# Latent attention: full-row rope scores on zero-padded keys, rotated queries by a second product, lag-table inputs on GpSimd, the softmax scale on the keys

## The chip, the cores and the metric

The kernel runs on one core of a Trainium2 chip. Its engines are TensorE (PE in the profile; its weight loads have rows of their own, PEld), VectorE (DVE), ScalarE (ACT), GpSimd (POOL) and SyncE (SP), whose queue issues most of the DMAs. The metric is device microseconds (us) of one execution; a kernel's time is the median of its runs.

## What is computed

The reference is a backbone of two layers over 512 latent tokens and 256 context tokens, 1024 features wide. Layer 0 is attention with 16 heads on a compressed key of 128 features and a rotary key of 64; layer 1 is a bidirectional diagonal state-space layer (S5) with a gated unit. Only the attention, and the part of the S5's preparation that runs beside it, are touched:

```python
scale = (MLA_NOPE + MLA_ROPE) ** -0.5
keys_lat = jnp.concatenate([ckv_l, _apply_rope(kr_l, cos, sin)], axis=-1)
keys_ctx = jnp.concatenate([ckv_c, kr_c], axis=-1)
q_pos  = jnp.concatenate([qa, _apply_rope(qr, cs[:, None], sn[:, None])], axis=-1)
q_free = jnp.concatenate([qa, qr], axis=-1)
s_all = jnp.concatenate([q_pos @ keys_lat.T, q_free @ keys_ctx.T], axis=-1)
p = jax.nn.softmax(s_all.astype(jnp.float32) * scale, axis=-1)
o = p[..., :s] @ ckv_l + p[..., s:] @ ckv_c
```

A latent query sees all 768 keys, the latent ones with rotated rope features and the context ones with plain ones; a context query sees the 256 context keys.

## The kernel before

**Precision.** Each float32 operand is split into a high and a low part (`split`, line 63: ACT copies, DVE subtracts), and a product is three matmuls (`mm3`, line 79: high by high, high by low, low by high).

**Attention.** Scores have queries on the partitions. A unit is 128 latent queries of one head, or its 256 context queries: five units a head, 80 units. For a unit of latent queries `score` (line 725) makes one group of five matmuls against 512 latent keys and one against 256 context keys; for one of context queries, two groups against 256 keys. In a group, lines 735 to 737 are the three products with the compressed key, line 738 is the rope product high by high, and line 739 the rope products high by low and low by high in one matmul, since the 64 rope features' high part lies in one half of the 128 partitions and their low part in the other (K1, K2 for the keys, `stack` for the queries). Line 738 therefore uses 64 partitions of both operands. `softmax` (line 741) takes the row maximum on DVE, multiplies it by minus the scale on ACT, takes the exponential on ACT with the scale, and divides, on DVE or ACT. `turn` transposes the probabilities on PE and splits them; `values` and `up_values` make the outputs.

**Queries.** `prep(h)` makes the operands of the next head in the units of the one before: `abs_steps` the compressed queries, and for every second head `rope_steps` (line 435) the rope queries of a pair of heads: one product `up`, an ACT copy to SBUF, eight DMAs on SP's queue that exchange blocks of 16 rows (`turn_rows`, line 423), three DVE operations with the cosine and sine tables, and splits.

**S5 beside the attention.** In units 1 to 51, 32 times (5 chunks in 8 units), `s5_chunk` (line 314) makes the state-out weights of four groups with six POOL products of 512 columns (lines 325 to 330), the inputs of the lag table with three DVE operations, a DVE memset and two ACT copies (lines 336 to 344), the lag table with 32 small matmuls (lines 348, 351), and stores it with eight DMAs on SP's queue (lines 357, 358). The inputs `cb` and the weights `wo` have two buffers each, `bk` one. From unit 52 on `win_early` (line 381) has POOL make 14 pieces of state-in weights: per piece two loads, six products (lines 372 to 377) and a store, in the buffers of `wo` and `pw`.

**Order.** The program is written in the order of the units; a scheduler (`schedule_with_timeline_sim`) puts the instructions of each engine and queue into an order by its own estimate of their times, and each engine runs its order strictly.

**After the attention** comes the output projection, whose weights `wload` loads through SP's queue (line 889).

Of the kernel before, what the change touches and what calls it, by code (L numbers as in the profile page):

```python
# [31 lines left out]
def hybrid_mla_s5(ctx, tc, I, O):  # L32
# [30 lines left out]
    def split(hi, lo, src):  # L63
        return act.copy(hi, src).ins, dve.tensor_sub(lo, src, f(hi)).ins  # L64
# [23 lines left out]
    def mod_steps(blocks, wt, ps, work, n):  # L88
        """rows of 512 columns of the modulation, block j in column group j: one step for each of the inputs' tiles"""
# [69 lines left out]
    def s5_params(take, mm):  # L159
# [102 lines left out]
        # (lam_bar - 1) / lam  # L262
# [16 lines left out]
        # powers: slot s holds lam_bar^s forward, lam_bar^(7-s) backward; state-in coefficients  # L279
        # coef * lam_bar * slot(7 - i), groups on the partitions, conjugated  # L280
# [33 lines left out]
    def s5_chunk(work, mm, c, pw, cci, half, dcol, eyek):  # L314
        """state-out weights and lag tables of groups 4c .. 4c+3"""
# [16 lines left out]
        # input weights of the lag table, the directions in separate columns  # L332
# [3 lines left out]
        dve.tensor_tensor(b1, bb, cci[:, 0:2, gs].rearrange("p r g -> p g r").unsqueeze(3).broadcast_to([P, 4, 2, 16]),  # L336
                          op=ALU.mult)
        dve.tensor_tensor(b2, bb[:, :, ::-1, :], cci[:, 2, gs].unsqueeze(2).unsqueeze(3).broadcast_to([P, 4, 2, 16]),
                          op=ALU.mult)
# [14 lines left out]
        act.copy(ks, o)  # L354
        dve.scalar_tensor_tensor(ks[:, 0:16], eyek, dcol[:, c:c + 1], ks[:, 0:16], op0=ALU.mult, op1=ALU.add)
# [25 lines left out]
    def win_early(tables, scratch, engs, more):  # L381
        """pieces made ahead and kept in DRAM: the last one is stored, the next one loaded, this one made"""
# [13 lines left out]
    # ================= layer 0: latent attention =================  # L396
    with ExitStack() as ctx_:
# [37 lines left out]
        def rope_steps(hp):  # L435
            st = {}

            def load():
                raw = qp(0)[:, :256]
                sp.dma_start(out=raw, in_=I["uqr"][hp])  # L440
                st["w"] = lw[0]("whi"), lw[0]("wlo")
                split(*st["w"], raw)
# [3 lines left out]
            def up(a, b):  # L446
                wh, wl = st["w"]
                o = lmm[0](b - a)
                for kc in range(2):
                    k = slice(kc * P, (kc + 1) * P)  # L450
                    mm3(o, wh[:, k], wl[:, k], Qh[kc][:, a:b], Ql[kc][:, a:b], kc == 0, kc == 1)
# [15 lines left out]
            def turned():  # L467
                (_, p0), (_, p1) = ropes[hp]
                q, t = st["q"], st["t"]
                dve.tensor_mul(q, q, cs[:, 0, :])  # L470
                dve.tensor_mul(t, t, cs[:, 1, :])
                dve.tensor_add(q, q, t)
                stack(q, p0, p1, slice(0, TL))
            return [plain, plain_ctx, turned]

        def abs_steps(h):
            st = hd.setdefault(h, {})

            def fold():
# [3 lines left out]
                split(*st["u"], wa[:, 384:512])  # L483
# [23 lines left out]
        with mkpool(name="in_h", bufs=KC) as hp, mkpool(name="in_w", bufs=3) as wp, \  # L507
# [5 lines left out]
            lmm[0], lw[0] = mm, lambda n: wp.tile([P, 1024], F32R, name=n)[:, :256]  # L513
# [14 lines left out]
            def mod_part(q):  # L528
                """shift and scale of 256 features, the even and the odd tiles of the inputs apart"""
# [74 lines left out]
            def rms(tiles, cols, n):  # L604
                """RMSNorm over the partitions of the tiles, in place"""
# [55 lines left out]
            dve.tensor_add(kr[:, 0:TL], kr[:, 0:TL], tmp)  # L661
            next(gate0)
# [5 lines left out]
            dve.tensor_copy(Ch, ckv)  # L668
            dve.tensor_sub(Cl, ckv, f(Ch))
            for j in range(2):  # L670
# [4 lines left out]
                split(Vh[:, 3 * j:3 * j + 3, :], Vl[:, 3 * j:3 * j + 3, :], tp)  # L675
            for i in range(2):
# [15 lines left out]
            def mod_more():  # L692
                """a step of the products with the modulation weights, and the loads for the next one"""
# [19 lines left out]
        with mkpool(name="at_s", bufs=2) as work, mkpool(name="at_p", bufs=2, space=PSUM) as ps, \  # L713
# [5 lines left out]
            lmm[0], lw[0] = mm, lambda n: work.tile([P, 256], F32R, name=n, bufs=1)  # L719

            # a unit is 128 latent queries of a head, or its 256 context queries
# [3 lines left out]
            def score(i):  # L725
# [3 lines left out]
                half, kx, kh = (lo_, K2, K1) if h % 2 == 0 else (up_, K1, K2)  # L729
# [741 lines left out]
```

## Time and profile before

| | |
|---|---|
| three runs | 1840.08, 1857.38, 1853.53 us; median 1853.53 us |
| profiled execution | span 1848.7 us from its first to its last instruction; no other time of it is given |
| busy in the span | PE 1653.3 us (89%), DVE 1137.1 (62%), ACT 694.6 (38%), POOL 683.2 (37%) |
| chain that ended last | PE 53%, DVE 21%, DMA 14%, ACT 3%, POOL 3% of the span |
| attention | from 265 us (first score, line 735) to 765 us (last product of `up_values`) |
| gates before it | 110 to 264 us |

The busy share is an average over stages: POOL works mainly in the attention and in the S5, DVE hardest in the attention. The chain goes back from the last instruction, at each step to what released it; its shares say which engine or transfer was last, not how busy it was. An engine's idle time counts only where something behind it waits. Matmuls are pipelined and their ends are modelled, so their cost is read from the distance of their starts.

### The profile page before, as it was taken

Reading aid. Unit: us, or ns where it says so; the run is one execution under the profiler, and the core shown is the slowest. Engines: PE = TensorE matmul, PEld = TensorE weight load, DVE = VectorE, ACT = ScalarE, POOL = GpSimd, SP = SyncE. Lnnn points to the kernel's source line nnn. Section 1 sums busy time; section 2 is a strip of 40 time slices with the busy share of each in tenths; the row PEclk is TensorE's granted clock in tenths of the full one; section 3 lists DMA queues with packets and bytes.
Section 4 is the critical chain, followed back from the end, with each engine's and each line's share of the span. In section 5 each row is a group of like instructions: output and inputs, shape, how many; then the busy total and the mean of one; then the engine's idle time right before and its main releaser. Section 6 shows DMA issues by size and latency. Waiting matters only on the chain.

```text
span 1848.7 us, 26973 instructions
## 1 busy us (share of the span) xinstructions
PE 1653.3 (89%) x9754; PEld 1321.5 (71%) x9754; DVE 1137.1 (62%) x2356; ACT 694.6 (38%) x1415; POOL 683.2 (37%) x788
## 2 busy tenths in 40 slices
PE   7999998888988989987899875687979999999997
PEld 4755787766766767766779765565768888888876
DVE  3864448888899677735551499998844332333347
ACT  2511226465565646611334332233454222222220
POOL 0000017666776477445105664626770000000022
PEclk8999999899999989998999887888989999999999
DMA  9366412222222455467647755339995333333352
GB/s 324 99 211 203 112 52 88 74 92 83 85 70 90 136 164 166 145 204 219 202 133 211 165 134 153 119 91 266 258 288 156 129 108 105 112 98 119 105 180 68
DMA packets 144244, 268.82 MB, mean 145 GB/s; under 512 B 39760, under 2 KB 74848, under 8 KB 143984
## 3 DMA queue, kind: packets, MB, share of 16 engines
q1 hardware_dynamic: 126256, 258.69, 46.9%
q10 hardware_dynamic: 17792, 8.39, 1.6%
q8 instruction: 77, 1.26, 0.3%
q14 instruction: 55, 0.45, 0.1%
q0 software_dynamic: 64, 0.03, 0.0%
HBM read 215.39 MB, written 49.30 MB: 143 GB/s over the span
## 4 chain that ended last, share of the span: by engine, by line
PE 53%; DVE 21%; DMA 14%; ACT 3%; issue 3%; POOL 3%; SPq 1%; DVEq 0%; ACTq 0%; POOLq 0%
PE mm L80 13%; PE mm L81 13%; PE mm L82 13%; DMA wraw<-in_wout_dram 3%; DVE st L1141 3%; DVE rt L1138 3%; DMA pt<-pind 3%; DVE st L1140 2%; DVE rt L1139 2%; PE modps L102 2%; PE sc L739 2%; PE sc L738 2%; DVE wlo L64 2%; DMA toe<-kd 2%; PE tr L775 2%
## 5 line engine op out<-in xcount | busy, mean ns | idle before, releaser
L64 DVE TENSOR_TENSOR wlo<-wraw,whi 128x1024 fp32r<-128x1024 f32 (+1 forms) x155 | 184.2, 1190 | 349.1 <-ACT whi L64 347.8
L64 ACT CAST whi<-wraw 128x1024 fp32r<-128x1024 f32 (+1 forms) x155 | 148.9, 962 | 467.5 <-PE mm L81 302.9
L81 PE MATMUL mm<-st,whi 128*128 128x512 f32 x512 | 201.6, 394 | 0.0
L80 PE MATMUL mm<-st,whi 128*128 128x512 f32 x512 | 201.3, 393 | 0.4 <-DVE t L1250 0.4
L82 PE MATMUL mm<-st,wlo 128*128 128x512 f32 x512 | 198.9, 388 | 0.0
L1333 POOL TENSOR_TENSOR x<-x,row_g 128x1024 f32<-128x1024 f32 x4 | 9.6, 2402 | 426.2 <-DMA x<-x1d 387.1
L80 PE MATMUL mm<-h,whi 128*128 128x512 f32 (+1 forms) x384 | 142.7, 372 | 11.6 <-DVE gg L1178 7.1
L325 POOL TENSOR_TENSOR wt<-cb,pw 128x512 f32<-128x512 f32 x32 | 36.3, 1133 | 301.5 <-DVE mx L752 268.3
L82 PE MATMUL mm<-h,wlo 128*128 128x512 f32 (+1 forms) x384 | 140.1, 365 | 6.4 <-DVE wlo L64 6.4
L81 PE MATMUL mm<-h,whi 128*128 128x512 f32 (+1 forms) x384 | 140.2, 366 | 0.8 <-DVE h L1034 0.8
L1093 PE MATMUL mm<-u,pt 128*128 128x96 f32 x512 | 73.1, 307 | 54.9 <-DMA u<-ud 36.5
L80 PEld LDWEIGHTS mm<-st,whi 128*128 128x128 f32 x512 | 96.1, 188 | 23.6 <-PE mm L82 0.8
L1093 PEld LDWEIGHTS mm<-u,pt 128*128 128x128 f32 x512 | 70.0, 221 | 58.2 <-issue 34.6
L82 PEld LDWEIGHTS mm<-st,wlo 128*128 128x128 f32 x512 | 96.1, 188 | 21.5
L81 PE MATMUL mm<-hl,whi 128*128 128x512 f32 (+1 forms) x320 | 109.9, 345 | 0.4 <-DVE hl L570 0.4
L81 PEld LDWEIGHTS mm<-st,whi 128*128 128x128 f32 x512 | 96.3, 188 | 19.1
L80 PE MATMUL mm<-hh,whi 128*128 128x512 f32 (+1 forms) x320 | 108.2, 346 | 1.7 <-ACT whi L64 1.7
L82 PE MATMUL mm<-hh,wlo 128*128 128x512 f32 (+1 forms) x320 | 108.9, 344 | 0.2 <-DVE wlo L64 0.2
L372 POOL TENSOR_TENSOR t<-pt,bt 128x512 f32<-128x512 f32 x14 | 20.8, 1488 | 223.8 <-DMA pt<-pind 177.4
L749 DVE TENSOR_REDUCE mx<-sc 128x1 f32<-128x768 f32 (+1 forms) x96 | 74.0, 772 | 37.4 <-PE sc L739 37.3
L775 PE MATMUL tr<-ident,p 128*128 128x128 f32 x448 | 72.2, 283 | 26.3 <-DVE ptl L64 22.7
L80 PEld LDWEIGHTS mm<-h,whi 128*128 128x128 f32 x384 | 75.4, 197 | 24.3 <-DVE gg L1178 7.9
(350 smaller groups left out, 4532.8 us busy)
## 6 DMA issues: line engine op xcount, KB each, us to landing
wraw<-in_wglu_dram SPq DMA_DIRECT2D x64, 512.0 KB
wraw<-in_win_dram SPq DMA_DIRECT2D x52, 512.0 KB
wod<-wo SPq DMA_DIRECT2D x32, 512.0 KB
wo<-wod SPq DMA_DIRECT2D x32, 512.0 KB
pt<-wid SPq DMA_DIRECT2D x24, 512.0 KB
u<-ud SPq DMA_DIRECT2D x32, 384.0 KB
pt<-pind SPq DMA_DIRECT2D x18, 512.0 KB
bt<-in_Bc_dram SPq DMA_DIRECT2D x18, 512.0 KB
```

The lines of the kernel that those rows point to most:

```text
L64: return act.copy(hi, src).ins, dve.tensor_sub(lo, src, f(hi)).ins
L80: pe.matmul(ps, lh, rh, start=first, stop=False)
L81: pe.matmul(ps, lh, rl, start=False, stop=False)
L82: pe.matmul(ps, ll, rh, start=False, stop=last)
L102: pe.matmul(mps[32 * j:32 * j + 2, :], sT[:, kc, :], w, start=(kc == 0), stop=(kc == KC - 1))
L738: pe.matmul(o, xr[half, ts], kh[half, a:b], start=False, stop=False)
L739: pe.matmul(o, xr[:, ts], kx[:, a:b], start=False, stop=True)
L749: dve.reduce_max(mx[:, 0:1], s, axis=AX.X)
L775: pe.transpose(tp[:, n, :], p[:, j * P:(j + 1) * P], ident)
L1093: pe.matmul(o[:, r, 96 * q:96 * (q + 1)], wi[:, q, r, :], us[m][:, 4 * (c % 2) + q, :], start=True, stop=True)
L1138: eng.tensor_tensor(t1, st[:, :, :, k], lr, op=ALU.mult)
L1141: eng.tensor_tensor(st[:, :, :, k + 1], st[:, :, :, k + 1], t2, op=ALU.add)
```

## The change

- The scale is multiplied into the rotary key and, after its use as value, into the compressed key. `softmax` takes the negated maximum on DVE and has no ACT multiplication.
- Two tiles KZ hold the high part of the rotary key in one half of the partitions and zeros in the other; line 738 becomes a matmul over all 128 partitions.
- The weights of the rope queries are stored twice in DRAM, as they are and with the blocks of 16 features exchanged. The rotated queries are a second product `up(0, TL, True)`; the copy to SBUF and the eight DMAs a pair of heads go, and the three DVE operations and the splits read PSUM. The load of these weights is twice as wide (512 columns).
- The low parts of the rope weights and of the head's value weights are made by POOL (`split(..., pool)`).
- In `s5_chunk` the two products of the lag table's input go to POOL, and two POOL additions of 64 partitions write `bk`, of which there are two, zeroed once. `half` and the two ACT copies go. The lag table's copy leaves out its first 16 columns, which DVE takes from PSUM.

```diff
+    def split(hi, lo, src, eng=None):
+        return act.copy(hi, src).ins, (eng or dve).tensor_tensor(lo, src, f(hi), op=ALU.subtract).ins
...
-        dve.tensor_tensor(b1, bb, cci[:, 0:2, gs]..., op=ALU.mult)
-        dve.tensor_tensor(b2, bb[:, :, ::-1, :], cci[:, 2, gs]..., op=ALU.mult)
-        dve.tensor_tensor(b1, b1, b2, op=ALU.add)
-        bk = work.tile([P, 4, 2, 48], F32, name="bk", bufs=1)
-        dve.memset(bk[:, :, :, 32:48], 0.0)
-        for d in range(2):
-            act.activation(bk[:, :, :, 16 * d:16 * d + 16], b1, AF.Copy, scale=half[:, d:d + 1])
+        pool.tensor_tensor(b1, bb, cci[:, 0:2, gs]..., op=ALU.mult)
+        pool.tensor_tensor(b2, bb[:, :, ::-1, :], cci[:, 2, gs]..., op=ALU.mult)
+        bk = bks[c % 2]
+        for d, rows in enumerate((lo_, up_)):
+            pool.tensor_tensor(bk[rows, :, :, 16 * d:16 * d + 16], b1[rows], b2[rows], op=ALU.add)
...
-        act.copy(ks, o)
-        dve.scalar_tensor_tensor(ks[:, 0:16], eyek, dcol[:, c:c + 1], ks[:, 0:16], op0=ALU.mult, op1=ALU.add)
+        act.copy(ks[:, 16:P], o[:, 16:P])
+        dve.scalar_tensor_tensor(ks[:, 0:16], eyek, dcol[:, c:c + 1], o[:, 0:16], op0=ALU.mult, op1=ALU.add)
...
             def load():
-                raw = qp(0)[:, :256]
+                raw = qp(0)
                 sp.dma_start(out=raw, in_=I["uqr"][hp])
-                split(*st["w"], raw)
+                split(*st["w"], raw, pool)
...
-                st["q"], st["t"] = qp(1), qp(0)
+                st["q"] = qp(1)
                 o = up(0, TL)
-                act.copy(st["q"], o)
-                turn_rows(st["t"], st["q"])
-                stack(st["q"], f0, f1, slice(0, TL))
+                stack(o, f0, f1, slice(0, TL))
+                dve.tensor_mul(st["q"], o, cs[:, 0, :])
...
-                q, t = st["q"], st["t"]
-                dve.tensor_mul(q, q, cs[:, 0, :])
-                dve.tensor_mul(t, t, cs[:, 1, :])
-                dve.tensor_add(q, q, t)
-                stack(q, p0, p1, slice(0, TL))
+                o = up(0, TL, True)
+                dve.tensor_mul(o, o, cs[:, 1, :])
+                dve.tensor_add(o, o, st["q"])
+                stack(o, p0, p1, slice(0, TL))
...
-                split(*st["u"], wa[:, 384:512])
+                split(*st["u"], wa[:, 384:512], pool)
...
+            dve.tensor_scalar_mul(kr, kr, SCALE)
...
-            dve.tensor_copy(Ch, ckv)
-            dve.tensor_sub(Cl, ckv, f(Ch))
...
+            dve.tensor_scalar_mul(ckv, ckv, SCALE)
+            dve.tensor_copy(Ch, ckv)
+            dve.tensor_sub(Cl, ckv, f(Ch))
...
-                half, kx, kh = (lo_, K2, K1) if h % 2 == 0 else (up_, K1, K2)
+                kx, kz = (K2, KZ[0]) if h % 2 == 0 else (K1, KZ[1])
...
-                    pe.matmul(o, xr[half, ts], kh[half, a:b], start=False, stop=False)
+                    pe.matmul(o, xr[:, ts], kz[:, a:b], start=False, stop=False)
...
-                    dve.reduce_max(mx[:, 0:1], s, axis=AX.X)
-                    act.mul(mx[:, 1:2], mx[:, 0:1], -SCALE)
-                    act.activation(p[:, a:b], s, AF.Exp, bias=mx[:, 1:2], scale=SCALE, accum_out=mx[:, 2:3])
+                    dve.reduce_max(mx[:, 1:2], s, axis=AX.X, negate=True)
+                    act.activation(p[:, a:b], s, AF.Exp, bias=mx[:, 1:2], scale=1.0, accum_out=mx[:, 2:3])
...
+            KZ = [work.tile([P, T], F32R, name=f"kz{i}", bufs=1) for i in range(2)]
+            for kz, k, rows, rest in ((KZ[0], K1, lo_, up_), (KZ[1], K2, up_, lo_)):
+                pool.memset(f(kz)[rest], 0.0)
+                act.copy(kz[rows], f(k)[rows])
+            bks = [work.tile([P, 4, 2, 48], F32, name=f"bk{i}", bufs=1) for i in range(2)]
+            for bk in bks:
+                pool.memset(bk, 0.0)
...
-    A["uqr"] = cont(ur.reshape(2, P, 8, P).transpose(2, 1, 0, 3).reshape(8, P, 256))
+    ur = ur.reshape(2, P, 8, 8, 16)
+    ur = np.stack([ur, ur[:, :, :, np.arange(8) ^ 1]], 0)
+    A["uqr"] = cont(ur.transpose(3, 2, 0, 1, 4, 5).reshape(8, P, 512))
```

## Rows read from the trace of the kernel before

**Rows 1.** Windows: stretch, length; busy PE, PEld, DVE, ACT, POOL; clock; DMA share, GB/s.
```profile
110.00:264.00 154.00, 153.77 (x761) 100.85 (x760) 67.10 (x188) 34.73 (x71) 0.00 (x0) 1.00 0.49 143
264.00:600.00 336.00, 296.40 (x2478) 233.32 (x2478) 291.67 (x545) 189.94 (x527) 235.03 (x192) 0.95 0.26 84
600.00:765.00 165.00, 152.89 (x949) 122.92 (x948) 113.40 (x227) 95.79 (x249) 113.74 (x85) 0.95 0.51 150
```

**Rows 2.** Timeline of PE's matmuls in the second unit: start, duration, what.
```profile
267.68 0.40 PE L736 MATMUL sc<-Cl,qd 128*128 128x512 f32 x1
267.91 0.39 PE L737 MATMUL sc<-Ch,qd 128*128 128x512 f32 x1
268.23 0.49 PE L738 MATMUL sc<-K,xp 64*128 64x512 f32 x1
268.65 0.50 PE L739 MATMUL sc<-K,xp 128*128 128x512 f32 x1
268.99 0.28 PE L735 MATMUL sc<-Ch,qd 128*128 128x256 f32 x1
269.11 0.28 PE L736 MATMUL sc<-Cl,qd 128*128 128x256 f32 x1
269.22 0.28 PE L737 MATMUL sc<-Ch,qd 128*128 128x256 f32 x1
269.43 0.38 PE L738 MATMUL sc<-K,t 64*128 64x256 f32 x1
269.75 0.38 PE L739 MATMUL sc<-K,t 128*128 128x256 f32 x1
269.97 0.27 PE L487 MATMUL mm<-wmod 128*128 128x128 f32 x1
```

**Rows 3.** The same windows view, from POOL's first to its last S5 product.
```profile
271.20:601.00 329.80, 290.20 (x2448) 229.43 (x2448) 289.93 (x541) 187.65 (x521) 235.91 (x192) 0.95 0.25 81
```

**Rows 4.** Groups by line, POOL: busy, mean ns, idle before and its releasers.
```profile
L327 POOL TENSOR_TENSOR wo<-wt,wt 128x512 f32<-128x512 f32 x32 | 42.9, 1340 | 55.5 <-issue 36.4 <-PE mm L351 14.3 <-DMA wod<-wo 2.0
...
L325 POOL TENSOR_TENSOR wt<-cb,pw 128x512 f32<-128x512 f32 x32 | 36.3, 1133 | 301.5 <-DVE mx L752 268.3 <-DMA cb<-in_CB_dram 31.5
```

**Rows 5.** Groups by line, POOL: its smaller products and sums in layer 1.
```profile
L1125 POOL TENSOR_TENSOR tr<-tr,trb 128x256 f32<-128x256 f32 x8 | 6.8, 856 | 0.5
...
L1128 POOL TENSOR_TENSOR tr<-tr,tr 128x128 f32<-128x128 f32 x8 | 3.7, 462 | 0.5
...
L1123 POOL TENSOR_TENSOR tr<-tr,lamt 128x128 f32<-128x128 f32 x8 | 3.3, 417 | 0.5
```

**Rows 6.** Groups by line, DVE: the operations of `s5_chunk`.
```profile
L340 DVE TENSOR_TENSOR b<-b,b 128x128 f32<-128x128 f32 x32 | 27.7, 867 | 0.3
...
L338 DVE TENSOR_TENSOR b<-cb,cci 128x128 f32<-128x128 f32 x32 | 23.5, 736 | 0.1
...
L355 DVE SCALAR_TENSOR_TENSOR ks<-eyek,dcol,ks 128x16 f32<-128x16 f32 x32 | 22.9, 715 | 0.7 <-ACT ks L354 0.5
...
L336 DVE TENSOR_TENSOR b<-cb,cci 128x128 f32<-128x128 f32 x32 | 22.5, 703 | 0.8 <-ACT bk L344 0.8
```

**Rows 7.** View of single lines: duration ns min/median/max, first and last start.
```profile
L336 DVE TENSOR_TENSOR b<-cb,cci x32: 278/607/1377, 272.7 to 596.6; 128x128 f32<-128x128 f32 x32
...
L426 SPq DMA_DIRECT2D modrow<-modrow x64: 507/587/1522, 229.8 to 704.9; - x64
...
L430 ACT CAST t<-modrow x8: 605/622/641, 229.6 to 700.5; 64x512 fp32r<-64x512 f32 x8
```

**Rows 8.** Timeline of POOL: first and last product of the 14 pieces.
```profile
615.42 1.29 POOL L372 TENSOR_TENSOR wt<-wo,pw 128x512 f32<-128x512 f32 x1 [14.54 <-DMA kd<-ks]
...
761.73 1.31 POOL L377 TENSOR_TENSOR wo<-pw 128x512 f32<-128x512 f32 x1
```

**Rows 9.** Timeline of SP's queue at the end of the attention.
```profile
763.06 0.33 SPq L386 DMA_DIRECT2D wid<-wo  x1
763.44 1.25 SPq L889 DMA_DIRECT2D wraw<-in_wout_dram  x2
```

More of the change, by code (lines that the diff above doesn't have):

```diff
@@ L61, in hybrid_mla_s5 @@
     pool.dma_start(out=nrm, in_=I["nrm"])
-    def split(hi, lo, src):
-        return act.copy(hi, src).ins, dve.tensor_sub(lo, src, f(hi)).ins
+    def split(hi, lo, src, eng=None):
+        return act.copy(hi, src).ins, (eng or dve).tensor_tensor(lo, src, f(hi), op=ALU.subtract).ins
     def wsplit(wp, src, n=1024):
@@ L312, in s5_params, with s5_chunk @@
             sp.dma_start(out=lamd[:, l], in_=lt[l])
-    def s5_chunk(work, mm, c, pw, cci, half, dcol, eyek):
+    def s5_chunk(work, mm, c, pw, cci, bks, dcol, eyek):
         gs = slice(4 * c, 4 * c + 4)
@@ L335, in s5_chunk @@
         bb = cb[:, :, :, 16:32]
[L336 to L339, printed above, removed]
[L340 to L344 removed]
+        pool.tensor_tensor(b1, bb, cci[:, 0:2, gs].rearrange("p r g -> p g r").unsqueeze(3).broadcast_to([P, 4, 2, 16]),
+                           op=ALU.mult)
+        pool.tensor_tensor(b2, bb[:, :, ::-1, :], cci[:, 2, gs].unsqueeze(2).unsqueeze(3).broadcast_to([P, 4, 2, 16]),
+                           op=ALU.mult)
+        bk = bks[c % 2]
+        for d, rows in enumerate((lo_, up_)):
+            pool.tensor_tensor(bk[rows, :, :, 16 * d:16 * d + 16], b1[rows], b2[rows], op=ALU.add)
         o = mm(P)
@@ L438, in load, with up @@
             def load():
-                raw = qp(0)[:, :256]
+                raw = qp(0)
                 sp.dma_start(out=raw, in_=I["uqr"][hp])
                 st["w"] = lw[0]("whi"), lw[0]("wlo")
-                split(*st["w"], raw)
+                split(*st["w"], raw, pool)
                 ropes[hp] = [(t768(F32R), ls.tile([P, TL], F32R, name=f"xp{e}", bufs=2))
                              for e in range(2)]
-            def up(a, b):
-                wh, wl = st["w"]
+            def up(a, b, turn=False):
                 o = lmm[0](b - a)
                 for kc in range(2):
-                    k = slice(kc * P, (kc + 1) * P)
-                    mm3(o, wh[:, k], wl[:, k], Qh[kc][:, a:b], Ql[kc][:, a:b], kc == 0, kc == 1)
+                    k = (kc + 2 * turn) * P
+                    wh, wl = (w[:, k:k + P] for w in st["w"])
+                    mm3(o, wh, wl, Qh[kc][:, a:b], Ql[kc][:, a:b], kc == 0, kc == 1)
                 return o
@@ L717, in mm @@
                 return ps.tile([P, 512], F32, name="mm")[:, :n]
-            lmm[0], lw[0] = mm, lambda n: work.tile([P, 256], F32R, name=n, bufs=1)
+            lmm[0], lw[0] = mm, lambda n: work.tile([P, 512], F32R, name=n, bufs=1)
             units = [(h, u) for h in range(HEADS) for u in range(5)]
@@ L794, in up_values @@
                 un[i].clear()
-            half = work.tile([P, 2], F32, name="half", bufs=1)
-            sp.dma_start(out=half, in_=I["half"])
+            KZ = [work.tile([P, T], F32R, name=f"kz{i}", bufs=1) for i in range(2)]
[5 more added lines that the diff above has]
+                pool.memset(bk, 0.0)
             dcol = work.tile([P, NCH], F32, name="dcol", bufs=1)
@@ L829, in hybrid_mla_s5 @@
                 if 5 * i // 8 < n_s5 <= NCH:
-                    s5_chunk(work, mm, n_s5 - 1, pw, cci, half, dcol, eyek)
+                    s5_chunk(work, mm, n_s5 - 1, pw, cci, bks, dcol, eyek)
                 if i == len(units) - 8:
@@ L1429, in lay_out @@
     A["Bc"] = cont(b.transpose(3, 1, 2, 0))
-    half = np.zeros((P, 2), np.float32)
-    half[:64, 0] = 1
-    half[64:, 1] = 1
-    A["half"] = half
     dc = np.zeros((4, 2, 16, 32), np.float32)
```

2 lines of the change are left out of this document (1 added, 1 removed).

## The prediction

> **What bounds the kernel now.** I read the windows of the stages first. Before the attention PE is busy all the time (153.8 of 154.0 us, clock 1.00), and POOL does nothing. In 264 to 600, with the 32 S5 chunks, PE is busy 296 of 336 us, DVE 292, POOL 235: three engines near their limit. From 600 to 765 PE is (153 of 165 us), with DVE at 113 and POOL at 114 [rows 1].
>
> How much of PE's busy time is work is read from the timeline, by the starts. The three compressed-key products of a 256-column group start 0.12 us apart, those of a 512-column group 0.23. Line 738, with 64 partitions, starts 0.21 after line 737, line 739 starts 0.32 after 738, and the next matmul 0.22 after 739. With 512 columns these are 0.32, 0.42 and 0.34 [rows 2]. The 64-row matmul breaks the pipeline at its entry and exit.
>
> Third, POOL's groups. Between its first and its last S5 product lie 329.8 us, 235.9 of them busy [rows 3]. The rest is mainly 55.5 us at line 327, for a free `wo` buffer that PE's lag-table matmuls or a store release late, and 31.5 us for `cb` loads [rows 4]. So POOL is paced by the others today, with 94 us to spare.
>
> **The change part by part.**
>
> *Full-row scores.* Three steps of a 256-column group are 0.21 + 0.32 + 0.22 = 0.75 us and would be 3 x 0.12 = 0.36 as full-row neighbours: 0.39 saved. With 512 columns 0.32 + 0.42 + 0.34 = 1.08 against 0.69: 0.39 again [rows 2]. There are 64 groups of 512 (four units in 16 heads) and 64 + 32 = 96 of 256: 160 x 0.39 = 62 us of PE, 0.78 a unit.
>
> The row shows a full-row weight load hidden behind the matmul before it: line 736 starts 0.12 us after 735 with other weights' load between them [rows 2]. The Trainium skill, TensorE: Matmul & The Clock Gate, section Part 3 (The mechanism), says the opposite: a weight load overlaps matmuls in flight only where the row groups differ. By that rule full rows would be no shorter; the trace disagrees, and the sum goes by the starts.
>
> *Second product.* Six 512-column matmuls at 0.23 [rows 2]: 1.4 us for each of 8 pairs of heads, 11 us of PE. The 64 exchange DMAs at 0.59 us [rows 7] leave SP's queue: 38 us of issue, counted at nothing, as what stands behind them there (chunk stores, weight loads) waits mostly for other things. The wider load of rope weights is one DMA as before, a unit ahead.
>
> *DVE and ACT.* The three operations of the lag table's input are 27.7 + 23.5 + 22.5 = 74 us of DVE in the 292 [rows 1, 6]. One takes 0.28 us at its shortest, 0.61 at the median, 1.38 at most [rows 7], the excess being about one POOL operation of 1.1 [rows 4]: it waits for POOL. ACT loses the maximum's multiplication, two copies a chunk and one a head pair; it was at 190 of 336 [rows 1], so nothing is counted. What DVE's relief is worth lies in PE's waits, which POOL now caps, so it gets no term of its own.
>
> *POOL.* Each chunk gets four operations: two products and two sums, 128 columns. Nearest rows: 0.42 and 0.46 us; lowest bound a quarter of a 512-column one, 0.28; highest a 256-column one, 0.86 [rows 4, 5]. I take 0.42, 0.42, 0.46, 0.46 = 1.76, which is 56 us for 32 chunks (36 to 110). The low parts of weights add, while the chunks run, 11 heads x 0.42 and 5 pairs x 1.13 [rows 4, 5]: 10 us. POOL's work in the chunks is then 235.9 + 56 + 10 = 302 us. The wait at line 327 goes, since POOL is now late and PE early. Of the 31.5 us for `cb`, which queue on SP behind the lag-table stores, between none and all may stay; I take a third, 10, as the stores come sooner after their chunk when PE and DVE are early. Chunk stretch: 312 in place of 330, **18 us less**. PE's own work there falls by 52 x 0.78 - 5 x 1.4 = 34 us of 296, DVE's by 74 of 292, so both fit below POOL. POOL is late next.
>
> The Trainium skill, GPSIMD Engine Reference, section Engine selection, keeps two-input elementwise work on VectorE, being about twice as fast there. The rows agree only where DVE waits for nothing (0.28 against 0.42). By the rule the move would cost 0.14 an operation; here DVE's mean is 0.70 to 0.87.
>
> *After the chunks.* The 28 units left save PE 28 x 0.78 = 22 us less two products (2.8): 19. With the 18 above PE would end 37 us sooner. POOL's 14 pieces, however, take from 615.4 to 763.0, paced by loads and stores [rows 8]; behind 18 us of gain they get 5 x 0.42 + 2 x 1.13 = 4 us of weight parts: POOL ends 14 us sooner. The output projection's first weight loads stand in SP's queue 0.4 us behind the last piece's store [rows 9]. Bounds 14 and 37. I take the middle, **25 us less**, since head 0's operands are made beforehand and only some of what follows needs POOL's buffers.
>
> *Before the attention.* One second product, 1.4 us, falls where PE has no gaps [rows 1]. KZ can be written only when the stage's space is free; its copy of 64 x 768 is nearest to 0.62 us for 64 x 512 [rows 7], about 0.9, and PE has three matmuls (0.7) to cover it: 0 to 3 us, taken as 1.5. The scalings and the later split of the key lie beside PE's gate products, DVE being busy 67 of 154 [rows 1]: nothing; uncovered, three 768-column operations, 3 us. Together **3 us more**.
>
> Sum: 25 - 3 = 22 us less. The profiled span, 1848.7, lies 4.8 under the median; I take that distance as fixed: 1853.5 - 22 = **1831**. From the bounds of its terms (POOL 0.28 to 0.5 an operation, `cb` 0 to 20, end 14 to 37) this case's own range is 1816 to 1843.
>
> **The rivals.**
>
> *A. PE's saving comes through whole.* The scheduler lets the S5 chunks slip behind the units, and the output projection starts without POOL's last piece. For it: PE needs POOL only for the chunks' small matmuls. Against: each engine's order is strict. PE's 62 - 11 = 51 us less 3: 1805; with fewer waits on DVE some 10 more, 1795.
>
> *B. Nothing comes of it.* All 31.5 us of `cb` waits stay (302 + 31.5 = 333, +3), and POOL's pieces gate the end (+4), plus 3: 1853 + 10 = 1863; with half of the waits, 1848. For it: POOL's idle time before a chunk is of that kind [rows 4]; against: SP issues less.
>
> *C. Slower: POOL's small operations are dear.* Strides, 64-partition outputs and waiting for DVE bring one to 0.86 [rows 5]. The chunks then take 235.9 + 110 + 10 + 31 = 387 us, PE waits at line 348 for `bk`, and against 22 us saved later 387 - 330 + 3 - 19 = 41 remain: 1895. It decides from 0.6 an operation with all `cb` waits. Against: the same instruction was 0.42 to 0.46.
>
> *D. The rope matmuls get no shorter*, their weight loads staying exposed as today. PE then keeps its 296 us in the chunks and its 153 after them, and 11 us of products are added: 1853 to 1868 with the 3 us from before the attention. Rows 2 speak against it. It is what the rule named above from the Trainium skill (TensorE: Matmul & The Clock Gate, Part 3) would give.
>
> **How the numbers follow.** Forecast 0.47, A 0.25, B 0.17, C 0.07, D 0.04. About 1% (18.5 us) is what a measurement of this kernel can tell from no change. The forecast lies just past it: of its 0.47 I put 0.31 beyond and 0.16 within. Faster 0.31 + 0.25 = 0.56; within 1% 0.16 + 0.16 + 0.04 = 0.36; slower, C and a corner of B, 0.08. The range leaves out C and the far ends of A and B: 1798 to 1858.
>
> **What would show it.** Line 738 as 128 rows, with 0.12 and 0.23 between starts. Small POOL operations near 0.45 us; POOL over 90% busy while the chunks run, its wait at line 327 nearly gone, and PE waiting for it at line 348. DVE's share there under 70%. POOL's last piece 10 to 20 us sooner, at 743 to 753, and PE at the end of the attention waiting on what stands behind it. Wrong it would be if POOL still waits at line 327 (A), if `cb` waits grow (B), or if the small operations exceed 0.6 (C).

## The result and the profile after

The changed kernel takes 1807.62 us (median; 1801.37 to 1812.57, four runs) beside 1849.91 us for the kernel before on the same chip: ratio 0.976, 95% interval 0.973 to 0.979, some 42 us less. The forecast was 22 less, 1831. The direction holds, and so does the whole range (1798 to 1858); the size was half, and the time lies below the 1816 to 1843 that the forecast's own terms allowed. The profiled execution, 1805.28 us with a span of 1803.5, is 45.2 us shorter than the one before (span 1848.7).

Where those 45 us lie is read from five marks in both traces:

| stretch | before | after | gained | forecast |
|---|---|---|---|---|
| start to POOL's first S5 product | 271.2 | 268.3 | 2.9 | -3 |
| POOL's first to last S5 product | 329.8 | 297.0 | 32.8 | 18 |
| from there to the first output product whose weights `wload` brings (`whi`, line 80) | 167.4 | 158.0 | 9.4 | 7 |
| from there to the end | 1080.3 | 1080.2 | 0.1 | 0 |

First the windows of the same stages; the columns are those of [rows 1]:

```profile
110.00:262.00 152.00, 151.34 (x768) 101.25 (x768) 66.57 (x186) 34.26 (x70) 2.48 (x3) 1.00 0.49 147
262.00:566.00 304.00, 272.68 (x2623) 235.35 (x2624) 200.18 (x426) 172.93 (x420) 290.18 (x339) 0.99 0.29 94
566.00:720.00 154.00, 123.44 (x848) 111.32 (x839) 95.85 (x197) 80.62 (x192) 112.54 (x90) 0.90 0.53 153
...
268.30:565.30 297.00, 266.61 (x2582) 230.47 (x2581) 197.12 (x422) 168.43 (x413) 287.09 (x335) 0.99 0.28 90
```

The last row answers to [rows 3]. In this stretch PE and DVE were both 88% busy before, POOL 72%. Now POOL is at 97% (287 of 297 us), PE at 90% and DVE at 66%; PE's granted clock rose from 0.95 to 0.99. After the chunks PE is busy only 123 of 154 us.

PE's timeline, answering to [rows 2]:

```profile
268.92 0.39 PE L735 MATMUL sc<-Cl,qd 128*128 128x512 f32 x1
269.15 0.40 PE L736 MATMUL sc<-Ch,qd 128*128 128x512 f32 x1
269.38 0.39 PE L737 MATMUL sc<-kz,xp 128*128 128x512 f32 x1
269.61 0.40 PE L738 MATMUL sc<-K,xp 128*128 128x512 f32 x1
269.85 0.28 PE L734 MATMUL sc<-Ch,qd 128*128 128x256 f32 x1
269.96 0.28 PE L735 MATMUL sc<-Cl,qd 128*128 128x256 f32 x1
...
270.20 0.28 PE L737 MATMUL sc<-kz,t 128*128 128x256 f32 x1
270.32 0.28 PE L738 MATMUL sc<-K,t 128*128 128x256 f32 x1
```

The steps are 0.23 us with 512 columns and 0.12 with 256, as forecast. Between lines 736 and 737 the weights change from those of a compressed query to those of a rope query, and nothing is lost.

POOL's groups by line while the chunks run, answering to [rows 4, 5]:

```profile
L327 POOL TENSOR_TENSOR wo<-wt,wt 128x512 f32<-128x512 f32 x32 | 41.5, 1297 | 0.8
...
L325 POOL TENSOR_TENSOR wt<-cb,pw 128x512 f32<-128x512 f32 x32 | 36.6, 1142 | 4.2 <-DMA cb<-in_CB_dram 2.1
...
L342 POOL TENSOR_TENSOR bk<-b,b 64x128 f32<-64x128 f32 x64 | 30.3, 474 | 2.4
L336 POOL TENSOR_TENSOR b<-cb,cci 128x128 f32<-128x128 f32 x32 | 14.7, 459 | 0.9 <-DMA cb<-in_CB_dram 0.9
L338 POOL TENSOR_TENSOR b<-cb,cci 128x128 f32<-128x128 f32 x32 | 12.9, 402 | 0.0
```

The wait at line 327 fell from 55.5 to 0.8 us, that for `cb` from 31.5 to 3.0 (2.1 at line 325, 0.9 at line 336), and the four small operations are 0.40 to 0.47 us. Now PE waits for POOL at line 346 (view of waits: total, times, longest):

```profile
PEld mm L346 <- POOL wo L330: 18.6, 21, 2.0
...
PE mm L346 <- POOL wo L330: 13.1, 15, 1.8
```

After the chunks POOL's 14 pieces still stand last, and SP's weight loads behind them, as in [rows 8, 9]; first POOL's timeline, then SP's, then the longest waits from 566 to 720:

```profile
716.58 1.32 POOL L375 TENSOR_TENSOR wo<-pw 128x512 f32<-128x512 f32 x1
```

```profile
717.93 0.32 SPq L384 DMA_DIRECT2D wid<-wo  x1
718.30 1.25 SPq L893 DMA_DIRECT2D wraw<-in_wout_dram  x2
```

```profile
POOL wt L370 <- DMA wo<-pind: 25.9, 11, 4.5
...
PE mm L82 <- POOL ul L64: 16.9, 2, 13.1
```

### The profile page after: what moved, and what is told of

The parts are those of the page before. It is cut to its first block, busy times and chain, and to the rows that moved or that the text cites. A ratio compares the mean times of both kernels' runs of the same rounds, so it can differ in the third digit from the quotient of the medians.

```text
span 1803.5 us, 26884 instructions
## 1 busy us (share of the span) xinstructions
PE 1603.7 (89%) x9802; PEld 1318.2 (73%) x9802; DVE 1029.4 (57%) x2206; ACT 662.8 (37%) x1249; POOL 738.9 (41%) x944
## 4 chain that ended last, share of the span: by engine, by line
PE 48%; DMA 20%; DVE 14%; POOL 10%; issue 4%; ACT 3%; SPq 1%; DVEq 0%; POOLq 0%; ACTq 0%
PE mm L80 13%; PE mm L81 13%; PE mm L82 13%; DMA wraw<-in_wout_dram 5%; DMA wo<-pind 3%; DMA pt<-pind 3%; DVE st L1145 2%; DMA toe<-kd 2%; DVE st L1144 2%; DVE rt L1142 2%; PE modps L102 2%; DVE wlo L64 2%; DVE rt L1143 2%; DMA wid<-wo 1%; DMA wraw<-in_win_dram 1%
## 5 line engine op out<-in xcount | busy, mean ns | idle before, releaser
L1097 PE MATMUL mm<-u,pt 128*128 128x96 f32 x512 | 79.0, 323 | 52.1 <-DMA u<-ud 30.7
L1097 PEld LDWEIGHTS mm<-u,pt 128*128 128x128 f32 x512 | 75.8, 236 | 55.4 <-issue 29.3
L80 PEld LDWEIGHTS mm<-st,whi 128*128 128x128 f32 x512 | 96.1, 188 | 23.7 <-PE mm L82 0.8
L749 ACT ACTIVATE p<-sc,mx 128x768 f32<-128x768 f32 (+1 forms) x96 | 73.8, 768 | 50.0 <-DVE mx L748 49.5
L64 POOL TENSOR_TENSOR ul<-wmod,uh 128x128 fp32r<-128x128 f32 x16 | 7.7, 481 | 199.3 <-ACT uh L64 199.2
L80 PE MATMUL mm<-whi,vh 128*128 128x512 f32 x186 | 72.9, 416 | 16.9 <-ACT whi L64 15.8
```

The source lines that it names most:

```text
L64: return act.copy(hi, src).ins, (eng or dve).tensor_tensor(lo, src, f(hi), op=ALU.subtract).ins
L80: pe.matmul(ps, lh, rh, start=first, stop=False)
L749: act.activation(p[:, a:b], s, AF.Exp, bias=mx[:, 1:2], scale=1.0, accum_out=mx[:, 2:3])
L1097: pe.matmul(o[:, r, 96 * q:96 * (q + 1)], wi[:, q, r, :], us[m][:, 4 * (c % 2) + q, :], start=True, stop=True)
```

## The experiments

The theory I began with, **P**: POOL paces the changed chunk stretch, and it could get there because PE and DVE were both relieved. Rivals: **R1**, the gain is PE's alone; **R2**, it is DVE's alone. Ratios below are to the kernel before on the same chip; "against the changed kernel" is the distance of the ratios times 1850 us.

The table is what most of the verdicts rest on. It follows POOL from the start of the first S5 product to the end of the last. "Products" are lines 325 to 330, each record counted from the end of the one before, so that overlaps are not counted twice; "small" are the lag-input operations, "low parts" those of the weights.

| kernel | stretch us | products | small | low parts | idle | DVE busy |
|---|---|---|---|---|---|---|
| before | 329.6 | 235.9 | - | - | 93.7 | 0.88 |
| full rows alone | 314.8 | 236.5 | - | - | 78.3 | 0.90 |
| lag inputs on POOL alone | 347.6 | 229.0 | 57.2 | - | 61.4 | 0.63 |
| these two | 314.0 | 234.0 | 56.3 | - | 23.7 | 0.73 |
| second product alone | 320.8 | 229.1 | - | - | 91.7 | 0.84 |
| changed | 296.9 | 223.4 | 53.6 | 10.0 | 9.9 | 0.66 |
| changed, half rows back | 322.1 | 223.3 | 54.7 | 10.2 | 33.9 | 0.60 |
| changed, lag inputs on DVE | 350.2 | 228.1 | - | 10.3 | 111.7 | 0.80 |
| changed, exchange DMAs back | 318.0 | 230.5 | 56.5 | 9.4 | 21.6 | 0.67 |
| changed, exchange issued too | 313.9 | 221.2 | 54.6 | 11.4 | 26.7 | 0.64 |
| changed, lag sum once | 278.2 | 222.4 | 39.6 | 10.0 | 6.2 | 0.68 |

The products' time does not follow DVE's share: 223.4 us at 0.66 but 230.5 at 0.67, 228.1 at 0.80 but 229.0 at 0.63. It follows one kind of DVE operation, those that read two operands from SBUF (the lag inputs, the `ks` sum from SBUF, the rotation of exchanged queries, low parts of weights). Take each product's time above the median of its line in the changed kernel, and sum it over the products that overlap such an operation in the timelines:

| kernel | products that overlap one, of 192 | their sum above the median, us | the others' sum, us |
|---|---|---|---|
| before | 158 | 14.7 | 1.2 |
| full rows alone | 158 | 15.2 | 1.2 |
| lag inputs on POOL alone | 57 | 7.2 | 1.7 |
| these two | 78 | 11.1 | 2.9 |
| second product alone | 142 | 7.5 | 1.5 |
| changed | 0 | 0 | 3.3 |
| changed, lag inputs on DVE | 138 | 7.0 | 1.0 |
| changed, exchange DMAs back | 30 | 7.4 | 3.0 |

Two such products, and the DVE operations beside them, with the exchange back (POOL's timeline, then DVE's); in the changed kernel the medians of the two lines are 1.07 and 1.27 us:

```profile
369.19 1.55 POOL L329 TENSOR_TENSOR wt<-cb,pw 128x512 f32<-128x512 f32 x1
370.83 1.60 POOL L330 TENSOR_TENSOR wo<-wt,wt 128x512 f32<-128x512 f32 x1
```

```profile
368.70 1.08 DVE L468 TENSOR_TENSOR modrow<-modrow,cs 128x512 f32<-128x512 f32 x1
369.70 1.59 DVE L469 TENSOR_TENSOR modrow<-modrow,cs 128x512 f32<-128x512 f32 x1
```

One thing holds for all verdicts: the scheduler puts each kernel in order anew, so an edit also moves instructions that it does not name. Between the first score and the first `whi` product PE has 3472 matmuls in the changed kernel. The longest sequence of them that another kernel runs in the same order, by operation and tiles in the timelines, is all 3472 for the third `wo` buffer and 3466 for the piece stores, but 2959 to 3089 for half rows, lag inputs on DVE, low parts, exchange issued and lag sum once, and 2624 for exchange DMAs back. Those runs show an edit together with its new order; no run held the order fixed.

**Half rows back.**

```diff
-pe.matmul(o, xr[:, ts], kz[:, a:b], start=False, stop=False)
+pe.matmul(o, xr[half, ts], kh[half, a:b], start=False, stop=False)
```

> The changed kernel with one part undone: line 737 (the rope product high by high) uses 64 partitions again, and the two KZ tiles go. Theory P (POOL paces the changed attention, and reached that pace because DVE and PE were both relieved): PE has about 32 us of waits for POOL in the chunk stretch and about 30 us of idle time after it, so of the 62 us that come back some 40 hide there; 5 to 25 us slower than the changed kernel (1813 to 1833). Rival R1 (the whole gain is PE's 62 us): 40 us slower or more, 1848 and over. Rival R2 (the whole gain is DVE's relief): within 5 us of the changed kernel.

1840.53 us, ratio 0.995 (0.993 to 0.997), some 34 us more than the changed kernel. Its window from 264 to 595, and DVE's wait for the scores:

```profile
264.00:595.00 331.00, 311.79 (x2607) 240.70 (x2607) 197.45 (x423) 170.96 (x415) 289.74 (x336) 0.99 0.26 86
```

```profile
DVE mx L748 <- PE sc L738: 43.2, 50, 2.9
```

PE takes 39 us more in this stretch than in the changed kernel at the same clock; 52 units at the forecast's 0.78 would be 41. POOL does the same work and idles 34 us. So full rows are needed for the gain, and with half rows PE paces (312 of 331 us busy). The time lies between P and R1.

**Lag inputs on DVE.**

```diff
-pool.tensor_tensor(b1, bb, ...)      # likewise b2 and the two sums bk
+dve.tensor_tensor(b1, bb, ...)
```

> The changed kernel with the four operations of the lag table's input on DVE in place of POOL, nothing else changed. Theory P: POOL loses 58 us of work in the chunk stretch, DVE gets about 60 to 90 us back on 200 of 304 and waits for POOL's operations again; the stretch is then held by DVE and PE together near where it is: -10 to +15 us against the changed kernel. Rival R1: POOL was the only brake left, so 10 to 20 us faster. Rival R2: 30 to 45 us slower, close to the kernel before.

1876.77 us, ratio 1.015 (1.011 to 1.019): slower than the kernel before and some 72 us more than the changed kernel. P, with -10 to +15, missed, and R2's 30 to 45 was too small. The groups of DVE, and the window:

```profile
L342 DVE TENSOR_TENSOR bk<-b,b 64x128 f32<-64x128 f32 x64 | 53.7, 839 | 3.5 <-PE mm L346 2.5
L338 DVE TENSOR_TENSOR b<-cb,cci 128x128 f32<-128x128 f32 x32 | 29.5, 921 | 0.0
L336 DVE TENSOR_TENSOR b<-cb,cci 128x128 f32<-128x128 f32 x32 | 24.2, 757 | 3.9 <-DMA cb<-in_CB_dram 3.7
```

```profile
264.00:620.00 356.00, 283.53 (x2491) 246.39 (x2490) 284.67 (x530) 161.57 (x396) 240.31 (x210) 0.89 0.24 78
```

The four operations are 107 us on DVE and 58 on POOL. Nobody is near its limit any more, PE's clock is down to 0.89, and POOL idles 112 us. The Trainium skill, GPSIMD Engine Reference, section Engine selection, gives such two-input work to VectorE; beside a busy POOL the measurement decides against it.

**Full rows alone, and lag inputs on POOL alone**, each in the kernel before.

```diff
-pe.matmul(o, xr[half, ts], kh[half, a:b], start=False, stop=False)
+pe.matmul(o, xr[:, ts], kz[:, a:b], start=False, stop=False)
```

> The kernel before with the full-row rope product on zero-padded keys alone. Theory P: DVE stays at 290 of 336 us in the chunk stretch and holds PE and POOL there; 10 to 25 us faster than the kernel before. Rival R1: 40 us faster or more. Rival R2: within 5 us of the kernel before.

1833.62 us, ratio 0.991 (0.988 to 0.994): 16 us less, as P expected; R1 and R2 are out.

```diff
-dve.tensor_tensor(b1, ...); dve.tensor_tensor(b2, ...); dve add; ACT copies into bk
+pool.tensor_tensor(b1, ...); pool.tensor_tensor(b2, ...); two pool sums into bk
```

> The kernel before with the lag table's input made by POOL alone (two products and two sums; the three DVE operations, the DVE memset and the two ACT copies go). Theory P: DVE falls by 70 us or more, PE's 62 us of broken pipeline stay and hold the stretch; 5 to 20 us faster than the kernel before. Rival R1: no faster than the kernel before. Rival R2: 30 to 45 us faster.

1864.62 us, ratio 1.008 (1.005 to 1.011): 15 us more. P missed this one, and so did R2; only R1's "no faster" holds. Windows of the two, and what was waited for in each:

```profile
264.00:600.00 336.00, 280.69 (x2642) 245.12 (x2641) 295.96 (x572) 200.02 (x555) 238.11 (x195) 0.94 0.27 88
```

```profile
PE tr L775 <- DVE ptl L64: 26.6, 18, 4.1
```

```profile
264.00:620.00 356.00, 323.03 (x2524) 245.07 (x2524) 221.01 (x427) 178.01 (x470) 285.42 (x320) 0.92 0.24 80
```

```profile
POOL wt L325 <- DMA cb<-in_CB_dram: 28.8, 5, 9.6
...
POOL bk L342 <- PE mm L346: 26.5, 10, 6.8
```

With full rows alone DVE stays at 296 of 336 us and PE waits for it. With the lag inputs alone PE stays at 323 of 356, and POOL waits for `cb` and for PE's release of `bk`.

**Both together, without the rest.** The two edits above in one kernel.

> The kernel before with two parts of the change: full-row scores and the four lag-input operations on GpSimd; no second product, no scale on the keys, low parts of the weights still on DVE. Theory I (the two parts need each other: each relieves one of PE and DVE, and only together does the wait not move to the other): 1805 to 1820, though the two parts alone gave -15 and +16. Rival S (the smaller parts carry a share of their own, 15 us or more): 1825 to 1840. Rival sum (parts add): 1848.

1826.39 us, ratio 0.985 (0.982 to 0.988): 28 us less. The two parts, -16 and +15 alone, are -28 together: they do need each other. But 16 us to the changed kernel are still missing, so the time is rival S's and not theory I's: something smaller carries a share.

**Exchange DMAs back.**

```diff
-o = up(0, TL, True); dve.tensor_mul(o, o, cs[:, 1, :]); dve.tensor_add(o, o, st["q"])
+turn_rows(st["t"], st["q"]); dve mul q; dve mul t; dve add      # shortened
```

> The changed kernel with the rotated queries made by the 64 exchange DMAs again and without the second product. Theory I (GpSimd paces the chunks, SP's issues are hidden, and so are 11 us of PE): 1800 to 1812, no change. Rival S (SP's 38 us of issue and the longer chain to the rotated queries count): 1820 to 1830.

1826.09 us, ratio 0.984 (0.981 to 0.987), some 14 us more than the changed kernel. S again: without the second product that share is gone. POOL's products are 7.1 us longer here, its idle time 11.7.

**Second product alone**, in the kernel before.

> The kernel before with the second product in place of the 64 exchange DMAs, and nothing else. Theory B (once in each pair of heads DVE is full for some 15 us while it turns the queries, PE waits for its probabilities and falls to the lower clock; the second product takes three operations on SBUF operands and the wait for the exchange out of that): 5 to 15 us less than before. Rival PE (PE is near its limit, so 11 us of products come on top): 0 to 11 us more.

1862.91 us, ratio 1.005 (1.003 to 1.008): 10 us more, inside rival PE's 0 to 11. Its mechanism is not shown, though: the chunk stretch is 8.8 us shorter than before (320.8 against 329.6), and the stretch from there to the first `whi` product 15 us longer (182.6 against 167.5), with 4 us more of PE's work in it. So the same part loses 10 us there and is worth 14 here. The burst that theory B named is in the kernel before (windows of 5 us, one of its head pairs), but taking the exchange out of it did not make this kernel faster:

```profile
515.00:520.00 5.00, 1.25 (x5) 0.74 (x6) 4.97 (x9) 2.27 (x6) 3.83 (x3) 0.91 0.14 29
520.00:525.00 5.00, 5.00 (x47) 4.30 (x48) 4.92 (x8) 0.86 (x3) 2.87 (x2) 0.50 0.02 5
```

DVE is full, PE stands for most of 5 us, and its granted clock in the next 5 is 0.50, the lower level, 1.2 GHz.

**Exchange issued, unused.** The changed kernel, second product and all, that also issues the 64 DMAs.

```diff
 dve.tensor_mul(st["q"], o, cs[:, 0, :])
+turn_rows(qp(0), st["q"])
```

> The changed kernel, second product and all, with the 64 exchange DMAs issued as well from the same place; nothing reads what they write. Theory Q (SP's queue is what the exchange costs: loads and stores of the chunks stand behind its issues): 10 to 15 us more than the changed kernel, about the 1826 of the run with the exchange in place of the product. Rival B (what costs is the rotation's longer chain on ACT and DVE, not SP's issues): 0 to 4 us more.

1829.23 us, ratio 0.989 (0.985 to 0.992), some 22 us more: above Q's 10 to 15, and rival B's 0 to 4 is out. Nothing computes with what they move. Window, POOL's line 325, and a wait of ACT:

```profile
269.20:583.00 313.80, 279.36 (x2601) 237.36 (x2599) 199.38 (x428) 170.41 (x420) 287.08 (x335) 0.97 0.27 88
```

```profile
L325 POOL TENSOR_TENSOR wt<-cb,pw 128x512 f32<-128x512 f32 x32 | 35.9, 1121 | 19.1 <-DMA cb<-in_CB_dram 17.1
```

```profile
ACT whi L64 <- DMA modrow<-in_uqr_dram: 19.1, 5, 5.3
```

POOL's work is the same to 0.1 us and its stretch is 16.8 us longer: its wait for `cb` at line 325 is 17.1 instead of 2.1, and 15.0 of that are three waits of 4.6 to 5.5 us. The last of the three, first SP's timeline, then POOL's:

```profile
548.66 4.93 SPq L424 DMA_DIRECT2D modrow<-modrow  x8
...
558.57 0.34 SPq L331 DMA_DIRECT2D wod<-wo  x1
558.95 0.43 SPq L318 DMA_DIRECT2D cb<-in_CB_dram  x1
```

```profile
557.28 1.26 POOL L330 TENSOR_TENSOR wo<-wt,wt 128x512 f32<-128x512 f32 x1
563.50 1.11 POOL L325 TENSOR_TENSOR wt<-cb,pw 128x512 f32<-128x512 f32 x1 [4.96 <-DMA cb<-in_CB_dram]
```

The eight exchanges hold SP's queue for 4.93 us, but that is over at 553.6. What the `cb` stands behind is the store of the chunk that POOL ends at 558.54: SP issues it 0.03 us later, and the next chunk's `cb` after it. So it is at all three waits, while in the changed kernel the next chunk's `cb` is always issued before the chunk's store. After the bursts at 367.74 and 426.7 us POOL waits for `cb` 1.2 us at most. So Q is right that SP's queue is where most of it costs. The place of the `cb` in the queue's order, which the scheduler changed when the exchanges were added, is what POOL's three waits show; that the length of the bursts delays it is not shown. The transfers also hold the buffer that the next `uqr` load writes (ACT's wait above), so not all of the 22 us need be SP's.

**Lag sum once.**

```diff
-pool.tensor_tensor(bk[rows, ...], b1[rows], b2[rows], op=ALU.add)   # for both halves
+pool.tensor_tensor(b1, b1, b2, op=ALU.add)
+act.copy(bk[rows, ...], b1[rows])                                    # for both halves
```

> The changed kernel with the lag input's sum as one operation over 128 rows on GpSimd and its two 64-row halves placed by ACT copies: 32 x 0.45 = 14 us of GpSimd's work leave the chunk stretch, ACT gets 64 copies. If GpSimd paces that stretch (theory I): 8 to 14 us less than the changed kernel, 1793 to 1800. Rival PE (its 267 us and its own waits hold the stretch at 297): 1804 to 1810.

`b1` gets a second buffer with it. 1813.19 us, ratio 0.975 (0.970 to 0.980): no shorter, near rival PE's 1804 to 1810. Yet its chunk stretch, in a profiled run of 1817.19 us, is:

```profile
269.00:547.20 278.20, 254.78 (x2517) 222.48 (x2517) 190.44 (x402) 178.30 (x458) 271.95 (x302) 0.99 0.28 94
```

POOL's work is 15 us less and its stretch 19 us shorter, so POOL did pace it, and rival PE's reason is out. The stretch from PE's last lag-table matmul to the first `whi` product grew from 157.0 to 167.4 us: of the 19 us gained in one stage, 10 are given back in the next. What comes later is 11 us longer too, but no edit here touches that part, and it took 1069 to 1091 us over the profiled runs.

**Third `wo` buffer.**

```diff
-wo = work.tile([P, 4, 2, P], F32, name="wo", bufs=2)
+wo = work.tile([P, 4, 2, P], F32, name="wo", bufs=3)      # for the chunks and for the pieces
```

> The changed kernel with a third buffer wo. Theory W (the stretch after the chunks is as long as the chain of the 14 stored pieces, whose loads wait for the store that frees their buffer): a piece comes every 8 us rather than 10, and 10 to 20 us go: 1787 to 1798. Rival PE (its 123 us and its waits for the splits hold the stretch): 1804 to 1810.

1793.79 us, ratio 0.967 (0.964 to 0.969), some 18 us less than the changed kernel, as theory W said. The 14 pieces take 121.5 us rather than 140.1 (577.8 to 699.3, and 576.5 to 716.6), and the first `whi` product starts 14 us sooner; the chunk stretch is as it was (297.3), and so is PE's order. So the chain of pieces bounded the stretch after the chunks.

**Low parts back on DVE.**

```diff
-split(*st["w"], raw, pool)    # likewise the split of uh, ul
+split(*st["w"], raw)
```

> The changed kernel with the low parts of the weights on DVE again. If GpSimd paces the chunks (theory I), its 10 us there go, and after the chunks PE's waits of 17 us for ul; the chain of stored pieces still sets the end: 5 to 10 us less than the changed kernel. Rival (DVE pays for them by waiting for GpSimd, in the same bursts): 0 to 8 us more.

1821.3 us, ratio 0.984 (0.980 to 0.987), 13 us more than the changed kernel: neither theory. The chunk stretch is 8.5 us shorter (288.4), as P has it, but after the chunks PE waits for the last heads' weights, which stand on SP behind a piece's store:

```profile
PE mm L484 <- DMA wmod<-in_absw_dram: 15.7, 3, 9.7
```

**Third buffer with late splits on DVE and an early output-weight load; the same with the lag sum once.**

```diff
+split(..., pool if h < 11 else dve)      # pairs: pool if hp < 6 else dve
-if i == len(units) - 8:                  # load and split of the first output weights
+if i == len(units) - 9:                  # load
+if i == len(units) - 5:                  # split
```

> The changed kernel with a third wo buffer, the low parts of the last heads' weights (from head 11) on DVE, and the first output weights loaded four units before they are split. Theory W (after the chunks the chain of pieces, PE's 17 us for ul behind a piece and ACT's 10 us for that load hold the stretch of 154 us, PE's work being 123): 20 to 30 us less than the changed kernel. Rival (the third buffer has taken all there is): 10 to 16 less, as with the third buffer alone.

> The kernel of the run before this with the lag input's sum once on GpSimd and its halves placed by ACT. Theory I with W (GpSimd's 14 us leave the chunk stretch, and no chain behind it takes them back this time): 10 to 18 us less than the run before this. Rival PE (with 252 of 276 us busy in the chunks it has no more to give, and stretches what follows): 0 to 5 less.

1798.97 us (ratio 0.973, 0.968 to 0.977) and 1793.84 us (0.968, 0.963 to 0.973). Neither reached its theory; the first is no better than the third buffer alone. In it ACT still stands 12.2 us for the output weights.

**Piece stores from POOL's queue**, in the changed kernel, and in the last kernel above.

```diff
-sp.dma_start(out=wid[c], in_=pt)
+pool.dma_start(out=wid[c], in_=pt)
```

> The changed kernel with the stores of the 14 pieces issued from GpSimd's queue and no longer from SP's. Theory H (after the chunks each store waits at the head of SP's queue for GpSimd's piece, and the loads of the last heads' weights and of the first output weights stand behind it): 8 to 18 us less than the changed kernel. Rival (GpSimd's piece rate holds the stretch, its DMA issue comes on top): 0 to 10 more.

> The kernel with third wo buffer, late splits on DVE and the lag sum once, and the piece stores from GpSimd's queue. Theory H: no wait for the last weights is left and the stretch after the chunks is PE's work and little more, 125 to 132 us: 10 to 20 us less than that kernel's 1794. Rival: GpSimd's issue slows the pieces as much as SP gains, 0 to 5 us either way.

1831.54 us (ratio 0.987, 0.982 to 0.992) and 1808.83 us (0.977, 0.972 to 0.981): 19 and 15 us more than the kernels that they start from. Theory H fell, and the rivals' 0 to 10 and 0 to 5 were too small. POOL's timeline in the first shows why:

```profile
594.08 1.33 POOL L375 TENSOR_TENSOR wo<-pw 128x512 f32<-128x512 f32 x1
599.01 1.26 POOL L370 TENSOR_TENSOR wt<-wo,pw 128x512 f32<-128x512 f32 x1 [3.60 <-issue]
600.23 1.26 POOL L371 TENSOR_TENSOR wt<-wo,pw 128x512 f32<-128x512 f32 x1
601.43 0.59 POOL L384 DMA_DIRECT2D wid<-wo  x1
```

The piece is ready at 595.41 and its store is issued at 601.43, in the middle of the next piece. In the changed kernel SP waited at that point, and issued 0.03 us after the piece:

```profile
583.16 1.31 POOL L375 TENSOR_TENSOR wo<-pw 128x512 f32<-128x512 f32 x1
```

```profile
584.50 0.34 SPq L384 DMA_DIRECT2D wid<-wo  x1
```

**Third buffer with the lag sum once; and that with the output weights loaded six units earlier.**

> The changed kernel with the third wo buffer and the lag input's sum once on GpSimd, nothing else. Theory C (GpSimd paces the chunks and the chain of pieces the stretch behind them, so the two gains, 18 us and 14 us in the profiled runs, add): 1775 to 1785. Rival PE (after the chunks PE is the next to be late, as in the run with the lag sum alone, and most of one of the two is lost): 1788 to 1796.

> The kernel of the run before this with the first output weights loaded six units earlier, behind nothing of the last pieces; they are split where they were. Theory H (ACT stands 8 to 12 us for that load, and PE behind it): 6 to 12 us less than the run before this. Rival (PE waits there for something else as long): 0 to 3 less.

1790.14 us (ratio 0.966, 0.963 to 0.970) and 1789.69 us (0.967, 0.963 to 0.970). The gains do not add (rival PE's times), and the early load is worth nothing, though ACT's wait for it fell from 6.9 to 3.1 us. From 562 to 710 us PE is busy in the first of them:

```profile
562.00:710.00 148.00, 127.83 (x813) 114.14 (x812) 103.86 (x202) 86.78 (x197) 103.91 (x85) 0.93 0.50 161
```

The third buffer alone, or with the lag sum, is the fastest seen: about 3.4% under the kernel before, 1% under the changed one. These three, and the one at 1793.84, cannot be told apart.

## Why the prediction was half right

- **Full rows.** Right: 0.12 and 0.23 us a step, and 0.75 us a unit of PE by the half-rows run, against 0.78. The sentence of the Trainium skill, TensorE: Matmul & The Clock Gate, section Part 3 (The mechanism), that the prediction names, by which a weight load overlaps matmuls in flight only where the row groups differ, does not show in these rows; the section's opening also lets a load to the background weight buffer be pulled ahead, which the prediction left out and which the rows do not speak against. Rival D is out. One reading was off without harm: line 736 before loads the weights of 735 again, and the change to others is at 737, 0.11 us after it [rows 2].
- **POOL paces the chunks.** Right. It is busy 97%, the wait at line 327 is gone, PE waits at line 346, DVE is at 66%, and taking 15 us from POOL shortened the stretch by 19.
- **The sum for the chunk stretch, 312 us.** This is the step that failed: 297.0 was measured. The term that was mis-sized is POOL's old work: I carried its 235.9 us over from before, and the same 192 products took 223.4. The small operations came out at 53.6 us (56 forecast) and the low parts at 10.0 (10). The 12.5 us are the products that ran beside DVE operations with two SBUF operands: 158 of them, 14.7 us above the median, before, and none after (the others' 1.2 us became 3.3). Each of two parts takes about half: the second product alone brings the products to 229.1, the lag inputs' move alone to 229.0; full rows alone leave them at 236.5.
- **`cb`, 10 us.** Wrong as a term, right in the sum by luck. The waits for `cb` were 3.0 us; POOL's whole idle time was 9.9, for which the sum had nothing else.
- **The exchange DMAs, "counted at nothing".** Wrong. Issued and unused they cost 22 us, 16.8 of them in the chunk stretch, where POOL waits for a `cb` that then stands behind a chunk's store in SP's queue. The 38 us of issue are not what was paid.
- **"DVE's relief gets no term of its own".** Right for what POOL caps, wrong in that taking the operations with two SBUF operands from DVE shortens POOL's own work. Put back on DVE, the lag inputs make the kernel 72 us slower than the changed one; the products' 4.7 us are a small part of that, POOL's idle time of 111.7 the large one.
- **After the chunks.** The 7 us beyond the chunks' gain were 9.4. The bounds 14 and 37 for both together missed 42.2 because the chunks' 18 was 32.8: with that they would be 29 and 52. POOL's last piece ended at 717.9, not 743 to 753. That its chain sets the end is shown by the third buffer.
- **Before the attention.** 3 us more forecast, 2.9 less measured, in one profile each. Full rows alone put the first score 2.7 us later (267.6 against 264.9), the changed kernel 1.7 sooner (263.2), which fits the KZ copy's price if another part pays it back; that was not isolated. The second product puts it 1.9 us later alone (266.8) and 2.5 in the changed kernel (263.2 against 260.7 with the exchange back), somewhat above the 1.4 forecast.
- **The rivals.** The time, 1807.62, lies beside rival A's 1795 to 1805, but not by its mechanism, since POOL gates both stretches: that the total comes near A is chance. B's and C's conditions did not occur.

Open: why the stretch behind the chunks grows by 10 us when the chunks end sooner, why each attempt on its single waits moved it to another, and how much of the differences between runs is the scheduler's new order. That POOL's products are long beside DVE operations with two SBUF operands is shown by the overlaps in the eight kernels of the second table; the `ks` sum, one of those operations, has no run of its own.

## What to carry to other kernels

When an engine is to become the bound, don't carry its old busy time over: look which of its operations were long because a neighbour was working, at which of the neighbour's operations, and whether the change takes those away; the neighbour's busy share alone does not tell it. Where two or three engines are near their limit, the parts of a change don't add; the same part cost 10 us alone and gave 14 with the others. And read from a queue's order what the load that a paced engine needs stands behind (here the next chunk's `cb` behind the store of the chunk just made), not only how long the queue is busy. Where a scheduler orders the program, an edit changes more than the lines that it names: compare the orders before a difference is put down to the edit alone.

## What the runs showed of the hardware

- 192 POOL products of 128x512 took 235.9 us where 158 of them overlapped a DVE operation with two SBUF operands (before), and 223.4 where none did (changed), with DVE still 66% busy.
- The same four small operations cost 58 us on POOL and 107 us on DVE, with POOL at work beside them.
- DVE's add into `ks` (line 355 before, 353 after) fell from 715 to 224 ns when its operand came from PSUM rather than SBUF; this row was not isolated by a run of its own.
- A DMA store that SP issued 0.03 us after its piece was issued 6.0 us after it from the queue of the engine that makes the pieces, since there it stood in program order with the next piece.
